# Sums of squares of the head norms in two rounded parts, and gate rows spread by one pass over a high and a low part

## The chip, the cores and the metric

One core of one Trainium2 chip runs the whole program. The metric is the device time of one execution in microseconds (us), as the median of several runs. The engines are TensorE (PE in the profile, its weight loads PEld), VectorE (DVE), ScalarE (ACT), GpSimd (POOL) and SyncE (SP), which here issues nearly all DMAs.

## The reference, cut to what matters

The program is two transformer blocks in a row, on 512 tokens of width 1024. The change touches the places where a vector of one head is divided by its root mean square:

```
def rms_norm(x, g):
    xf = x.astype(jnp.float32)
    y = xf * lax.rsqrt(jnp.mean(xf * xf, axis=-1, keepdims=True) + EPS)
    return (y * g.astype(jnp.float32)).astype(x.dtype)
...
    q = rms_norm(q.reshape(b, nc, CHUNK, N_HEADS, HEAD_DIM), q_norm_g)
    k = rms_norm(k.reshape(b, nc, CHUNK, N_HEADS, HEAD_DIM), k_norm_g)
...
        q_sb = rms_norm_2(to_heads(q_sb, SB_HEADS), g_q_sb[l])
        k_sb = rms_norm_2(to_heads(k_sb, SB_HEADS), g_k_sb[l])
        y_sb = stick_breaking(q_sb, k_sb, to_heads(v_sb, SB_HEADS)).transpose(0, 2, 1, 3)
        y_sb = rms_norm_2(y_sb, g_out_sb[l])
...
        y_ml = rms_norm_2(y_ml.transpose(0, 2, 1, 3), g_out_ml[l]) * jax.nn.sigmoid(o_ml)...
```

The first block has a chunked attention with 16 heads of 64, a gated convolution and a feed-forward part. The second block has two mixers side by side: stick-breaking attention with 8 heads of 64, and an mLSTM with 4 heads of 128, whose weights come from one input gate and one forget gate per head and token. After them comes the PEER layer, which picks 16 of 16384 experts per head and token and is by far the longest part.

## The kernel before, in words

Activations lie with features on partitions and the 512 tokens along the free axis, so one tile is 128 by 512 and holds two heads of 64 or one of 128. Large products (`linear`, `linear2`, `rows_linear`, all through `mm3` at L153 to L155) are made of float32r passes over a rounded high part and a low rest: three matmuls for each product. A float32r operand is made by a cast on ScalarE (`nc.scalar.copy`) and its rest by a subtraction on VectorE or GpSimd (`split` at L180 and L181; `weights` at L142, L144, L148).

The head norms are the exception. `qk_norm` (L494 on) squares a query or key tile on ScalarE (L500, tile `qn_s`) and sums the squares over the 64 rows of each head with one plain float32 matmul against a block matrix of ones (L502, `bone`). `head_norm` (L798 on) does the same for the outputs of the second block's mixers (L803, L805), with `bone` for stick-breaking and a full matrix of ones for the mLSTM. The profile shows each of these float32 matmuls as two PE instructions. The sum lands in the PSUM bank `d`; `rsqrt` (L186 to L200) reads it into `rs_m`, takes Ln and Exp on ScalarE (tile `rs_r`), squares the result (tile `rs_q`) and makes one correction step on VectorE; L504 or L808 then applies it. The tiles `rs_m`, `rs_r`, `rs_q` and `qn_s` have one buffer each in these stages.

There are 32 such sums: four per group in the attention of the first block (4 groups: two query tiles, two key tiles), four per group in stick-breaking (2 groups), four output norms of stick-breaking and four of the mLSTM.

The mLSTM also needs two gate rows per head, spread over all 128 partitions. `gates` makes them for all four heads as tiles of 4 rows (`grow`, `frow`). `products` spreads one row with a float32 matmul against a 0/1 selector of 4 rows (`sel`), at L970 for `grow` and L1012 for `frow`: 8 matmuls in all.

The order of the instructions on each engine is fixed when the program is built: a scheduler of the framework lists them by when it reckons their inputs ready, taking the text's order as priority. On the chip each engine works through its list in that order, and an instruction whose input is late holds up the ones behind it. GpSimd has few jobs in the stages in question: copies of the halves of the q and k tiles (L514), clearing (L605, L922, L984) and the low parts of the mLSTM's q and k (L181).

Of the kernel before, what the change touches and what calls it, by code (L numbers as in the profile page):

```python
# [8 lines left out]
F32 = mybir.dt.float32  # L9
F32R = mybir.dt.float32r  # L10
F16 = mybir.dt.float16
U32 = mybir.dt.uint32
AF = mybir.ActivationFunctionType
# [8 lines left out]
P = 128  # L22
D = 1024
T = 512
# [19 lines left out]
V_QG, V_KG, V_QS, V_KS, V_OSB, V_OML, V_GB = 160, 161, 162, 163, 164, 168, 172  # L44
# [24 lines left out]
class Ker:  # L69
# [12 lines left out]
    def setup(self, es):  # L82
        nc, I = self.nc, self.I
        self.cp = es.enter_context(self.pool("cp"))
        self.raws = None
        self.table, self.table_load, self.table_users = None, None, []
        cst = self.cp.tile([P, 2 * P], F32, name="cst")
        nc.sync.dma_start(cst, I["consts"][:, 0:2 * P])
        vec = self.cp.tile([P, V_W], F32, name="vec")
        nc.sync.dma_start(vec, I["vecs"])  # L90
        self.vec = vec
        self.ident, self.bone = cst[:, 0:P], cst[:, P:2 * P]
        self.ones = self.cp.tile([P, P], F32, name="ones")
        nc.vector.memset(self.ones, 1.0)
        self.mod = self.cp.tile([P, 48], F32, name="mod")

    def act(self, out, x, func, **kw):
# [380 lines left out]
    def gains(self, vcol, mcol):  # L478
# [4 lines left out]
        self.gm = gm  # L483
        return gm

    def qk_in(self, tp, ps, rstd):

        q = tp.tile([P, T], F32, name="qn_n", bufs=2 if rstd is not None else 4)
        if rstd is None:
            self.nc.scalar.copy(q, ps)  # L490
        else:
            self.nc.vector.tensor_mul(q, ps, rstd)
        return q

    def qk_norm(self, tp, pool, q, gcol, tag, twice):


        nc = self.nc
        sq = tp.tile([P, T], F32, name="qn_s", bufs=1)
        nc.scalar.activation(sq, q, AF.Square)  # L500
        pn = self.psum("d" if "d" in self.nbanks else "b")
        nc.tensor.matmul(pn, self.bone, sq, start=True, stop=True)  # L502
        r = self.rsqrt(tp, pn, 1.0 / 64)
        nc.vector.scalar_tensor_tensor(q, q, gcol, r, op0=ALU.mult, op1=ALU.mult)  # L504
        out = []
        for f in range(2):
            own, other = slice(64 * f, 64 * f + 64), slice(64 - 64 * f, 128 - 64 * f)
            a = pool.tile([P, T], F32R, name=f"{tag}a{f}", tag=f"{tag}a{f}")
            nc.scalar.copy(a[own], q[own])
            if twice:  # L510
                b = pool.tile([P, T], F32R, name=f"{tag}b{f}", tag=f"{tag}b{f}")
                nc.vector.tensor_sub(b[own], q[own], a[own].bitcast(F32))
                for t in (a, b):
                    nc.gpsimd.tensor_copy(t[other], t[own])  # L514
                out.append((a, b))
            else:
                nc.vector.tensor_sub(a[other], q[own], a[own].bitcast(F32))
                out.append(a)
        return out
# [137 lines left out]
    def mix(self, es_x):  # L657
        from contextlib import ExitStack
        nc, I = self.nc, self.I
# [7 lines left out]
        tp = self.nq_pool  # L667
# [11 lines left out]
        with ExitStack() as es:  # L679
# [2 lines left out]
            cr = sp.tile([P, 7 * P], F32R, name="cr")  # L682
            self.mlc = sp.tile([P, P], F32, name="mlc")
            nc.sync.dma_start(self.mlc, I["consts"][:, C_MLM:C_MLM + P])
            self.sel = sp.tile([4, 4 * P], F32, name="sel")
            nc.sync.dma_start(self.sel, I["consts"][0:4, C_SEL:C_SEL + 4 * P])
            with self.pool("ci") as tp:
                ci = tp.tile([P, 4 * P], F32, name="ci")
                nc.sync.dma_start(ci, I["consts"][:, C_TRI:C_TRI + 4 * P])
                nc.scalar.copy(cr[:, P:2 * P], ci[:, 0:P])  # L690
                nc.scalar.copy(cr[:, 3 * P:6 * P], ci[:, P:4 * P])
            nc.scalar.copy(cr[:, 0:P], self.ident)
            nc.vector.tensor_scalar_mul(cr[:, 2 * P:3 * P], self.ones, -1.0)
            nc.scalar.copy(cr[:, 6 * P:7 * P], self.ones)
# [63 lines left out]
    def gates(self, sp, hs):  # L758

        nc, I = self.nc, self.I  # L760
        with self.pool("gt") as tp:
            raw = tp.tile([P, KO, P], F32, name="if_w")
            nc.sync.dma_start(raw, I["w_if"])
            hi = tp.tile([P, KO, P], F32R, name="if_h")
            lo = tp.tile([P, KO, P], F32R, name="if_l")
            nc.scalar.copy(hi, raw)
            nc.vector.tensor_sub(lo, raw, hi.bitcast(F32))
            ps = self.linear((hi, lo), 0, hs, tag="b")
            z = tp.tile([P, T], F32, name="if_z")
            nc.scalar.activation(z[:36], ps[:36], AF.Identity, bias=self.v(V_GB)[:36])  # L770
            f = tp.tile([4, T], F32, name="if_f")
            nc.vector.tensor_copy(f, z[32:36])
            e = tp.tile([4, T], F32, name="if_e")
            nc.scalar.activation(e, f, AF.Abs)
            self.act(e, e, AF.Exp, scale=-1.0)
            self.act(e, e, AF.Ln, bias=1.0)
            lf = tp.tile([4, T], F32, name="if_lf")
            nc.vector.scalar_tensor_tensor(lf, f, 0.0, e, op0=ALU.min, op1=ALU.subtract)
            one = tp.tile([4, T], F32, name="if_1")
            nc.vector.memset(one, 1.0)  # L780
            A = tp.tile([4, T], F32, name="if_A")
            nc.vector.tensor_tensor_scan(A, one, lf, 0.0, op0=ALU.mult, op1=ALU.add)
            b = tp.tile([4, T], F32, name="if_b")
            nc.vector.tensor_sub(b, z[0:4], A)
            grow = sp.tile([4, T], F32, name="grow")
            nc.vector.tensor_tensor_scan(grow, one, b, 0.0, op0=ALU.mult, op1=ALU.max)
            frow = sp.tile([4, T], F32, name="frow")
            nc.vector.tensor_add(frow, A, grow)
            self.act(frow, frow, AF.Exp, scale=-1.0)
            nc.vector.tensor_scalar_min(frow, frow, 1e18)  # L790
            pb = self.psum("b")
            for s in range(4):
                nc.tensor.transpose(pb[:, 4 * s:4 * s + 4], b[:, s * P:(s + 1) * P], self.ident[:4, :4])
            bt = sp.tile([P, 16], F32, name="bt")
            nc.vector.tensor_copy(bt, pb[:, :16])
        return bt, grow, frow

    def head_norm(self, tp, mp, y, ones, gcol, scale, eps=None, extra=None):  # L798


        nc = self.nc
        sq = tp.tile([P, T], F32, name="qn_s", bufs=1)
        nc.scalar.activation(sq, y, AF.Square)  # L803
        pn = self.psum("d")
        nc.tensor.matmul(pn, ones, sq, start=True, stop=True)  # L805
        r = self.rsqrt(tp, pn, scale, eps=eps)
        t = tp.tile([P, T], F32, name="hn_t", bufs=1)
        nc.vector.scalar_tensor_tensor(t, y, gcol, r, op0=ALU.mult, op1=ALU.mult)  # L808
# [4 lines left out]
    def stick_breaking(self, mp, hs, pq, pk):  # L813
        nc, I = self.nc, self.I
        widths = [512, 384, 256, 256]
        out = []
        with self.pool("sb") as tp, self.pool("sbq", bufs=2) as qp, self.pool("sbv", bufs=4) as vp:
# [53 lines left out]
            def head(g, j, f, qk, vs):  # L871
# [9 lines left out]
                    ys[g, j] = tp.tile([P, T], F32, name="sb_y", bufs=1)  # L881
                self.weigh_values(ys[g, j], f, self.psum("d"), vs, 2 * j + f, ws, widths)
                if f:
                    out.append(self.head_norm(tp, mp, ys[g, j], self.bone, self.v(V_OSB + 2 * g + j), 1.0 / 64))
                yield

            old = None
# [59 lines left out]
    def mlstm(self, mp, tp, qp, vp, ml, bt, grow, frow):  # L947
# [69 lines left out]
        def norm(h, pn, den):  # L1017
# [5 lines left out]
            self.act(l, l, AF.Ln, bias=1.0)  # L1023
            nc.vector.scalar_tensor_tensor(o, o, 0.0, l, op0=ALU.min, op1=ALU.subtract)
            self.act(o, o, AF.Exp)
            return self.head_norm(tp, mp, pn, self.ones, self.v(V_OML + h), 1.0 / P, den, o)

        for h in range(4):
            yield [norm(h, *products(h))]
# [498 lines left out]
```

## Time and profile before

| | |
|---|---|
| median of 3 runs | 2579.02 us (2578.01 to 2582.98) |
| profiled execution: its own time | 2575.19 us |
| profiled execution: span | 2573.4 us |
| mean granted TensorE clock | 0.992 |
| PE busy | 2489.6 us (97%) |
| DVE busy | 1898.0 us (74%) |
| ACT busy | 1100.5 us (43%) |
| POOL busy | 617.4 us (24%) |

The span runs from the first to the last instruction; the time of the profiled execution is 1.8 us longer. The attention of the first block lies at about 190 to 505 us, the second block's mixers at about 950 to 1290 us, and the PEER layer from there to the end. Matmuls are pipelined: an entry's duration holds the way through the array, so what one matmul costs PE is read from the distance between starts.

### The profile page before, as it was taken

How to read it: one execution, taken by the hardware profiler on the slowest of the kernel's cores; microseconds unless marked ns; L12 is line 12 of the kernel's file. 1: busy time of each engine (PE TensorE's matmuls, PEld its weight loads, DVE VectorE, ACT ScalarE, POOL GpSimd, SP SyncE). 2: the span in 40 equal slices, each digit the busy share in tenths (PEclk: the TensorE clock that was granted, in tenths of full speed). 3: DMA queues.
4: the chain of work that ended last, by engine and by line, in shares of the span. 5: the costliest groups of instructions: out<-in, count | busy, mean ns of one | idle time of the engine just before them, and what ended most of it. 6: DMA issues, size and time to landing. Idle time of an engine off the chain costs nothing.

```text
span 2573.4 us, 33226 instructions
## 1 busy us (share of the span) xinstructions
PE 2489.6 (97%) x12637; PEld 2118.3 (82%) x12637; DVE 1898.0 (74%) x3238; ACT 1100.5 (43%) x1479; POOL 617.4 (24%) x510
## 2 busy tenths in 40 slices
PE   8999999999999999999999979989999999999999
PEld 6887877877888878777788967868889999999998
DVE  5558777745555567887789989847767777888887
ACT  4226555633222247657643248733333333333332
POOL 0001110111001101101054420001135555555552
PEclk9999999999999999999999989989999999999999
DMA  5352222444444331134333357689879999999995
GB/s 194 128 203 95 101 86 99 170 150 142 161 164 147 131 119 67 58 105 142 131 121 109 119 183 275 266 274 348 298 262 328 326 332 328 328 333 331 331 332 192
DMA packets 172313, 515.04 MB, mean 200 GB/s; under 512 B 13396, under 2 KB 78308, under 8 KB 146296
## 3 DMA queue, kind: packets, MB, share of 16 engines
q1 hardware_dynamic: 133960, 376.52, 41.7%
q0 software_dynamic: 37040, 135.35, 14.6%
q8 instruction: 99, 1.62, 0.2%
q10 hardware_dynamic: 1152, 1.05, 0.1%
q14 instruction: 62, 0.51, 0.1%
HBM read 461.47 MB, written 51.38 MB: 199 GB/s over the span
## 4 chain that ended last, share of the span: by engine, by line
PE 76%; DVE 14%; ACT 5%; issue 2%; DMA 2%; POOL 1%; SPq 0%; DVEq 0%; ACTq 0%; POOLq 0%
PE pa L155 12%; PE pa L153 11%; PE pa L154 11%; PE pp L1417 7%; PE pp L1416 7%; PE pp L1420 7%; PE pu L153 4%; PE pu L155 4%; PE pu L154 4%; ACT whi L142 1%; DVE wlo L144 1%; DVE tk_rest L1187 1%; PE pb L588 1%; PE pc L608 1%; DMA mg_a<-g_dram 1%
## 5 line engine op out<-in xcount | busy, mean ns | idle before, releaser
L142 ACT CAST whi<-wraw 128x2048 fp32r<-128x2048 f32 x229 | 437.7, 1911 | 573.0 <-PE pa L154 295.7
L144 DVE TENSOR_TENSOR wlo<-wraw,whi 128x2048 fp32r<-128x2048 f32 x210 | 492.8, 2346 | 139.0 <-ACT whi L142 134.3
L155 PE MATMUL pa<-hh,wlo 128*128 128x512 f32 (+1 forms) x1360 | 521.8, 385 | 19.8 <-POOL wlo L148 17.2
L153 PE MATMUL pa<-hh,whi 128*128 128x512 f32 (+1 forms) x1360 | 526.4, 387 | 14.9 <-ACT hh L228 10.8
L154 PE MATMUL pa<-lh,whi 128*128 128x512 f32 (+1 forms) x1360 | 523.1, 385 | 0.0
L155 PEld LDWEIGHTS pa<-hh,wlo 128*128 128x128 f32 x1360 | 257.7, 190 | 65.0 <-POOL wlo L148 18.9
L153 PEld LDWEIGHTS pa<-hh,whi 128*128 128x128 f32 x1360 | 258.0, 190 | 61.9 <-ACT hh L228 11.3
L1416 PE MATMUL pp<-whi,hew 128*128 128x512 f32 x768 | 300.1, 392 | 6.4 <-ACT hew L1383 6.4
L1417 PE MATMUL pp<-wlo,hew 128*128 128x512 f32 x768 | 300.6, 392 | 1.6 <-DVE wlo L144 1.6
L1145 POOL DMA_INDIRECT r_row<-in_u_rows,r_at x128 | 186.0, 1453 | 479.5 <-DVE r_w L1166 447.3
L154 PEld LDWEIGHTS pa<-lh,whi 128*128 128x128 f32 x1360 | 258.0, 190 | 44.2 <-issue 6.5
L1420 PE MATMUL pp<-whi,lew 128*128 128x512 f32 x768 | 237.6, 391 | 0.0
L1145 POOL DMA_INDIRECT r_row<-in_expert_v,r_at x128 | 194.9, 1522 | 177.1 <-DVE r_big L1174 139.5
L153 PE MATMUL pu<-hh,whi 128*128 128x384 f32 x640 | 217.0, 339 | 0.0
L155 PE MATMUL pu<-hh,wlo 128*128 128x384 f32 x640 | 216.7, 339 | 0.0
L154 PE MATMUL pu<-lh,whi 128*128 128x384 f32 x640 | 216.3, 338 | 0.0
L1416 PEld LDWEIGHTS pp<-whi,hew 128*128 128x128 f32 x768 | 144.6, 188 | 35.7 <-ACT hew L1383 6.6
L1417 PEld LDWEIGHTS pp<-wlo,hew 128*128 128x128 f32 x768 | 144.4, 188 | 30.4 <-DVE wlo L144 2.5
L1420 PEld LDWEIGHTS pp<-whi,lew 128*128 128x128 f32 x768 | 144.5, 188 | 30.4
L1174 DVE SCALAR_TENSOR_TENSOR r_big<-r_row,r_w,r_big 128x1024 f32<-128x1024 f32 x127 | 162.9, 1283 | 3.0
L1383 ACT CAST hew<-ex_w 128x384 fp32r<-128x384 f32 x128 | 65.6, 513 | 228.3 <-DVE ex_w L1379 151.3
L1166 DVE CUSTOM_DVE_ANT_0 r_row<-r_row,r_big 128x1024 f32<-128x1024 f32 x128 | 151.4, 1220 | 0.0
(436 smaller groups left out, 4552.5 us busy)
## 6 DMA issues: line engine op xcount, KB each, us to landing
wraw<-in_expert_u SPq DMA_DIRECT2D x64, 1024.0 KB, 7.2
wraw<-in_expert_v SPq DMA_DIRECT2D x64, 1024.0 KB, 7.6
wraw<-in_w_in SPq DMA_DIRECT2D x37, 1024.0 KB, 4.8
ada_w<-in_w_ada SPq DMA_DIRECT2D x24, 1024.0 KB, 4.8
gate_dram<-oh_s SPq DMA_DIRECT2D x12, 2048.0 KB, 6.9
ex_g<-gate_dram SPq DMA_DIRECT2D x31, 768.0 KB, 9.9
wraw<-in_w_up SPq DMA_DIRECT2D x16, 1024.0 KB, 5.9
wraw<-in_w_down SPq DMA_DIRECT2D x16, 1024.0 KB, 4.8
```

The costliest lines, as they stand in the source:

```text
L142: nc.scalar.copy(hi, raw)
L144: nc.vector.tensor_sub(lo, raw, hi.bitcast(F32))
L153: mm(out, wh, xh, start=start, stop=False)
L154: mm(out, wh, xl, start=False, stop=False)
L155: return mm(out, wl, xh, start=False, stop=stop)
L1145: self.nc.gpsimd.indirect_dma_start(t, None, src, at)
L1166: later(nc.vector.tensor_tensor_reduce(row, row, h, 1.0, 0.0, op0=ALU.mult, op1=ALU.add, accum_out=w[:, k:k + 1]))
L1174: later(nc.vector.scalar_tensor_tensor(acc, row, w[:, k:k + 1], acc, op0=ALU.mult, op1=ALU.add))
L1383: nc.scalar.copy(hi, w)
L1416: mm(sums[b][half], hi, v[0][:, c, hc], start=n == 0, stop=False)
L1417: mm(sums[b][half], hi, v[1][:, c, hc], start=False, stop=False)
L1420: mm(sums[b][half], lo, v[0][:, c, hc], start=False, stop=n == P - 1)
```

## The change

Every sum of squares goes through a new method `sum_squares`: the squares (`qn_s`) are cast to float32r on ScalarE (`hi`), GpSimd subtracts to get the rest (`lo`), and two float32r matmuls add both parts in the bank. `hi` and `lo` take the buffers of `rs_m` and `rs_q`, which `rsqrt` uses afterwards. The matrices of ones are float32r copies (`boner`, new, made at the start; `onesr`, which was there). The two gate rows become tiles of 36 rows: the rounded rows on partitions 0 to 3, the rest on 32 to 35, zeros elsewhere, and the selector has ones at both places, so that one float32r matmul spreads a row.

```
@@ setup
+        self.boner = self.cp.tile([P, P], F32R, name="boner")
+        nc.scalar.copy(self.boner, self.bone)
...
+    def sum_squares(self, tp, q, ones, tag):
+        nc = self.nc
+        sq = tp.tile([P, T], F32, name="qn_s", bufs=1)
+        hi = tp.tile([P, T], F32R, name="qn_h", tag="rs_m")
+        nc.scalar.activation(sq, q, AF.Square)
+        nc.scalar.copy(hi, sq)
+        lo = tp.tile([P, T], F32R, name="qn_l", tag="rs_q")
+        nc.gpsimd.tensor_sub(lo, sq, hi.bitcast(F32))
+        pn = self.psum(tag)
+        nc.tensor.matmul(pn, ones, hi, start=True, stop=False)
+        nc.tensor.matmul(pn, ones, lo, start=False, stop=True)
+        return pn
@@ qk_norm
-        sq = tp.tile([P, T], F32, name="qn_s", bufs=1)
-        nc.scalar.activation(sq, q, AF.Square)
-        pn = self.psum("d" if "d" in self.nbanks else "b")
-        nc.tensor.matmul(pn, self.bone, sq, start=True, stop=True)
+        pn = self.sum_squares(tp, q, self.boner, "d" if "d" in self.nbanks else "b")
@@ mix
-            self.sel = sp.tile([4, 4 * P], F32, name="sel")
-            nc.sync.dma_start(self.sel, I["consts"][0:4, C_SEL:C_SEL + 4 * P])
+            self.sel = sp.tile([36, 4 * P], F32R, name="sel")
...
+                cs = tp.tile([36, 4 * P], F32, name="cs")
+                nc.vector.memset(cs, 0.0)
+                for p in (0, 32):
+                    nc.sync.dma_start(cs[p:p + 4], I["consts"][0:4, C_SEL:C_SEL + 4 * P])
+                nc.scalar.copy(self.sel, cs)
@@ gates
-            grow = sp.tile([4, T], F32, name="grow")
+            grow = tp.tile([4, T], F32, name="if_g")
...
-            frow = sp.tile([4, T], F32, name="frow")
+            frow = tp.tile([4, T], F32, name="if_r")
...
-        return bt, grow, frow
+            out = []
+            for n, x in (("g", grow), ("f", frow)):
+                both = sp.tile([36, T], F32R, name=f"{n}row")
+                nc.gpsimd.memset(both.bitcast(F32), 0.0)
+                nc.scalar.copy(both[0:4], x)
+                nc.vector.tensor_sub(both[32:36], x, both[0:4].bitcast(F32))
+                out.append(both)
+        return bt, *out
@@ head_norm
-        sq = tp.tile([P, T], F32, name="qn_s", bufs=1)
-        nc.scalar.activation(sq, y, AF.Square)
-        pn = self.psum("d")
-        nc.tensor.matmul(pn, ones, sq, start=True, stop=True)
+        pn = self.sum_squares(tp, y, ones, "d")
```

The callers of `head_norm` pass `boner` and `onesr` in place of `bone` and `ones`.

## Rows read from the trace of the kernel before

**Rows 1.** Busy time of each engine by stretch: attention, norms, stick-breaking, mLSTM.
```profile
core 0: us, PE busy (x) PEld busy (x) DVE busy (x) ACT busy (x) POOL busy (x), PEclk, DMA share, GB/s
190.00:505.00 315.00, 309.38 (x1633) 252.05 (x1632) 245.49 (x534) 180.66 (x353) 33.35 (x62) 1.00 0.31 107
950.00:1000.00 50.00, 49.94 (x268) 40.55 (x267) 36.08 (x50) 28.41 (x46) 7.27 (x10) 1.00 0.25 86
1000.00:1140.00 140.00, 129.41 (x676) 107.40 (x676) 124.44 (x210) 101.11 (x175) 9.37 (x13) 0.98 0.16 55
1140.00:1290.00 150.00, 142.58 (x692) 111.06 (x691) 112.32 (x166) 92.90 (x164) 12.60 (x14) 1.00 0.42 142
```

**Rows 2.** Tile qn_s: counts, duration ns min/median/max, first and last start.
```profile
L502 PE MATMUL pd<-qn_s,cst x48: 590/592/697, 196.8 to 1072.9; 128*128 128x512 f32 x48
...
L805 PE MATMUL pd<-qn_s,cst x8: 590/592/697, 1035.5 to 1134.4; 128*128 128x512 f32 x8
...
L805 PE MATMUL pd<-qn_s,ones x8: 590/592/594, 1193.5 to 1244.0; 128*128 128x512 f32 x8
```

**Rows 3.** Tile sel, in the same columns.
```profile
L970 PE MATMUL pg<-grow,sel x8: 587/640/692, 1170.0 to 1226.6; 4*128 4x512 f32 x8
```

**Rows 4.** Timeline of PE around one sum of the attention: start, duration, instruction.
```profile
363.29 0.39 PE L153 MATMUL pa<-hh,whi 128*128 128x512 f32 x1
363.54 1.13 PE L502 MATMUL pd<-qn_s,cst 128*128 128x512 f32 x2
364.10 0.80 PE L154 MATMUL pa<-lh,whi 128*128 128x512 f32 x1
364.74 0.39 PE L155 MATMUL pa<-hh,wlo 128*128 128x512 f32 x1
364.96 0.39 PE L153 MATMUL pa<-hh,whi 128*128 128x512 f32 x1
```

**Rows 5.** Timeline of PE around one sum of stick-breaking.
```profile
993.27 0.40 PE L153 MATMUL pa<-hh,whi 128*128 128x512 f32 x1
...
994.59 0.39 PE L155 MATMUL pa<-hh,wlo 128*128 128x512 f32 x1
```

**Rows 6.** Timeline of PE around one spread gate row.
```profile
1191.22 0.28 PE L155 MATMUL pa<-whi,lh 128*128 128x256 f32 x1
1191.43 1.12 PE L1012 MATMUL pd<-frow,sel 4*128 4x512 f32 x2
...
1192.70 0.28 PE L154 MATMUL pa<-wlo,hh 128*128 128x256 f32 x1
```

**Rows 7.** Groups by shape on POOL and ACT: busy, mean ns, idle before.
```profile
L181 POOL TENSOR_TENSOR lk<-ml_a,hk 128x512 fp32r<-128x512 f32 x4 | 6.1, 1514 | 22.0 <-ACT hk L180 21.8
L181 POOL TENSOR_TENSOR lq<-ml_a,hq 128x512 fp32r<-128x512 f32 x4 | 5.7, 1425 | 33.1 <-ACT hq L180 33.1
...
L180 ACT CAST hmx<-hn_t 128x512 fp32r<-128x512 f32 x8 | 5.0, 619 | 9.9 <-DVE hn_t L808 5.2 <-DVE hn_t L810 4.8
```

**Rows 8.** Waits of PE, 190 to 510 us: total, times, longest.
```profile
PE pd L502 <- ACT qn_s L500: 1.7, 5, 0.8
```

**Rows 9.** Waits of PE, 1140 to 1290 us.
```profile
PE ps L155 <- POOL lk L181: 0.7, 1, 0.7
PE ps L153 <- ACT hk L180: 0.6, 1, 0.6
```

**Rows 10.** Timelines of DVE and POOL beside each other near 997 us.
```profile
997.86 0.98 DVE L200 SCALAR_TENSOR_TENSOR rs_q<-rs_q,rs_r 128x512 f32<-128x512 f32 x1
...
1002.81 0.69 DVE L197 SCALAR_TENSOR_TENSOR rs_q<-rs_m,rs_q 128x512 f32<-128x512 f32 x1
...
997.34 1.97 POOL L514 CAST qb<-qb 64x512 fp32r<-64x512 f32 x2
```

**Rows 11.** Timeline of DVE: the norms of the first group of the attention.
```profile
211.93 0.68 DVE L189 TENSOR_SCALAR rs_m<-pd 128x512 f32<-128x512 f32 x1
212.53 0.74 DVE L504 SCALAR_TENSOR_TENSOR qn_n<-qn_n,gq,rs_q 128x512 f32<-128x512 f32 x1
...
219.99 0.74 DVE L504 SCALAR_TENSOR_TENSOR qn_n<-qn_n,vec,rs_q 128x512 f32<-128x512 f32 x1
```

**Rows 12.** Timelines of POOL and PE at the group's first scores.
```profile
223.21 1.63 POOL L514 CAST kb<-kb 64x512 fp32r<-64x512 f32 x2
...
227.65 0.28 PE L588 MATMUL pb<-ka,qa 128*128 128x256 f32 x1
```

More of the change, by code (lines that the diff above doesn't have):

```diff
@@ L883, in head @@
                 if f:
-                    out.append(self.head_norm(tp, mp, ys[g, j], self.bone, self.v(V_OSB + 2 * g + j), 1.0 / 64))
+                    out.append(self.head_norm(tp, mp, ys[g, j], self.boner, self.v(V_OSB + 2 * g + j), 1.0 / 64))
                 yield
@@ L1025, in norm @@
             self.act(o, o, AF.Exp)
-            return self.head_norm(tp, mp, pn, self.ones, self.v(V_OML + h), 1.0 / P, den, o)
+            return self.head_norm(tp, mp, pn, self.onesr, self.v(V_OML + h), 1.0 / P, den, o)
         for h in range(4):
```

## The prediction

> **What bounds the kernel now.** I read the busy times first, then the same by stretch, then the two tiles the change is about, then PE's timeline around single instructions, and last the waits. The reader should see in the stretches that PE is what every touched stage is full of: 309.4 of 315 us in the attention, 49.9 of 50 while the first norms of stick-breaking run, 142.6 of 150 in the mLSTM [rows 1]. Only the stretch from 1000 to 1140 is different: PE is busy for 129.4 of 140 us and DVE for 124.4, so there PE waits some 10.6 us for chains that run over DVE and ACT. After 1290 us nothing is changed; what comes before shifts it as a whole, so that a microsecond won or lost before 1290 counts in full.
>
> **What PE is spared.** There are 48 + 8 + 8 PE instructions for the sums [rows 2], two for each, so 32 sums; and 8 for one kind of gate row [rows 3], two for each of four heads, the other kind being the same again: 8 rows. The price of a float32 sum is read from starts. In the attention a float32r pass goes out every 0.22 to 0.23 us (364.74 to 364.96). From the pass ahead of the sum to the second pass behind it there are 1.45 us (363.29 to 364.74) [rows 4]; less two ordinary passes (0.46) the sum costs 0.99 us, its slow successor of 0.80 us included. In stick-breaking the same distance is 1.32 us [rows 5], so 0.86. The new form costs two passes, 0.46 us. Sixteen sums lie in the attention and sixteen in the second block: 16 x (0.99 - 0.46) + 16 x (0.86 - 0.46) = 8.5 + 6.4 = 14.9 us.
>
> A gate row takes 1.48 us from the short pass ahead (1191.22) to the second behind [rows 6]; less two short passes of half the columns (0.11 each, half of 0.23) that is 1.26. The new row is one pass, 0.23 us, but over 36 of 128 rows. The old one costs 0.27 to 0.40 more than a sum over all rows, so something may hang on the narrow shape and stay: 0.23 to 0.63. I take 0.5, since the new shape is nearly as narrow: 8 x 0.76 = 6.1 us (bounds 5.0 and 8.2). Together 21.0 us of PE work go away.
>
> **What is added.** Each sum gets a cast of 128x512 on ACT, 0.62 us, and a subtraction of 128x512 on POOL, 1.43 to 1.51 us by the low parts of the mLSTM's q and k [rows 7]. ACT's 32 x 0.62 = 20 us are spread over stages where it is busy for 57 to 72% [rows 1], and POOL's 32 x 1.47 = 47 us over stages where it has 7 to 15%. Their throughput is free; were ACT's cover gone, all 20 us would count. What is not free is the order. A sum's result used to be there 1.13 us after its square was [rows 4]; now it takes 0.62 + 1.47 and a last pass of 0.39, so 2.5 us, 1.35 us later.
>
> *Waits of PE for the new links.* PE now waits at the place of `hi` for ACT and at the place of `lo` for POOL. Queued behind are `linear`'s passes, which need nothing of it; they are the cover if the scheduler puts the passes late enough. No row shows this sum in two parts. Below, it costs nothing; above, if PE stood for both links, 2.1 us, 67 us in all. The nearest rows are the mLSTM's q and k: the same cast, the same subtraction on POOL, and PE passes that need them. There PE waited 0.7 us for POOL once and 0.6 for ACT once, in 8 such pairs [rows 9], 0.16 us for each. The square itself, in the attention, cost PE 1.7 us in 16 sums [rows 8], 0.11 each. I take 0.16: 32 x 0.16 = 5.1 us.
>
> *DVE beside POOL.* While POOL copies 64x512 (997.34 to 999.31), DVE's step at 997.86 takes 0.98 us; the same shape alone takes 0.69 [rows 10]: 0.29 longer. A subtraction of 1.47 us can lie beside two such steps, so up to 0.6 us of DVE. In the attention DVE has 70 us to spare [rows 1] and this hides. Between 1000 and 1140 it doesn't: four q and k norms and four output norms lie there, 8 x 0.6 = 4.6 us above, nothing below if they fall beside steps that don't suffer. I take the middle, 2.3 us.
>
> The page SBUF — State Buffer of the Trainium skill (section "Who interferes with whom") speaks against the change more strongly: DVE and GpSimd share a port pair as an exclusive lock, an instruction with two SBUF inputs on DVE contends with GpSimd's reads, and whoever is first blocks the other for a whole instruction. The trace shows 0.29 us where a whole copy would be about 1 us [rows 10], so it bears out the contention, not the full lock. By the rule the eight subtractions would hold DVE 8 x 1.47 = 11.8 us; by the row, 2.3 to 4.6.
>
> *The small edits.* `boner` is one ACT cast at the start, when ACT waits for the first inputs; `sel` gets one DMA more on SP, a memset and a cast, in a stretch where PE has its list full (49.9 of 50). The gate rows add one ACT cast and one DVE subtraction each ahead of the first spread, with some 0.62 + 0.69 us once by [rows 7, 10]; behind it are the mLSTM's first weights. Between 1140 and 1290 PE idles 7.4 us as it is, so between 0 and 1.3 us; I take 0. The POOL memsets come early.
>
> **Sum.** 21.0 - 5.1 - 2.3 = 13.6 us off the profiled 2575.19 us: 2561.6 us. The median of the runs lies 3.8 us above the profiled time, so I forecast 2579.0 - 13.6 = 2565.4 us, about 0.5% faster.
>
> **The rivals.** *All of it arrives.* If PE's list has room for every new link and DVE doesn't suffer, 21 us stay: 2558 us. For it speaks that PE is over 98% busy in the attention; against it, that between 1000 and 1140 a shorter PE has nothing to do with the spare time.
>
> *The norms queue up behind each other.* `hi` and `lo` sit in the one buffer of `rs_m` and of `rs_q`, and `rs_q` is free only when the norm ahead has been applied. Before, the first key's sum was read at 211.93, ahead of the end of the norm before it (212.53 + 0.74 = 213.27) [rows 11]. Now its low part can't be written before that norm is applied, which itself is 1.35 us later: 214.6, and with the subtraction and the pass the reading starts near 216.5, 4.6 us later. The rest of that norm took until 219.99, 8 us for some 4 us of steps, so up to 4 us may be caught up. The first scores start 2.8 us after the last copy they need (223.21 + 1.63 = 224.84 to 227.65) [rows 12]. If nothing is caught up, 1.8 us are lost in each of six groups, 11 us: 2565.4 + 11 = 2576 us, no change. Against it: V's products and gate products are there for PE to fill with, which is why I leave it out of the sum.
>
> *The full lock.* By the whole-instruction block the eight subtractions of the stretch 1000 to 1140 would cost 11.8 us of DVE, not 2.3: 2575 us, no change. This is the mechanism of the cited section; the rows speak for a fifth to two fifths of it.
>
> *Slower.* PE stands at `lo`. PE's list is written by the scheduler's reckoning; if that takes POOL for faster than it is, `lo` is listed too early and all passes behind it stand. The attention's four groups are in the same order, so one bad place comes four times. From 21.0 / 32 = 0.66 us per sum on, the change loses. With 1.0 us, less than the subtraction alone, PE stands for 32 us: 2579 + 32 - 21 = 2590 us. PE's wait of 0.8 us for a square [rows 8] shows that single waits of this size occur; that it was one in sixteen, and 0.16 us per pair with POOL [rows 9], speaks against it.
>
> **Chances.** The forecast 0.50 (2561 to 2573), all of it 0.15, the queue of norms 0.13, the full lock 0.07, slower 0.15. What a measurement here can tell from no change is about 0.2%, 5 us: below 2574 is faster, above 2584 slower. The two cases in the middle straddle that edge: I give 0.07 of their 0.20 to faster and 0.13 to no change. So faster 0.72, same 0.13, slower 0.15. The range reaches from a little under the full gain to what no change with a little stall gives, 2555 to 2581, and leaves out the slower case and a bit at either end.
>
> **What would show it.** In the changed kernel PE's starts around a high or low pass should lie 0.23 us apart with no slow successor. The attention should shrink by 5 to 8 us and the rest up to 1290 us by 6 to 12. The waits of PE should name POOL's subtraction (`qn_l`) with some 0.1 to 0.2 us per sum: over 0.66 us means the slower case. DVE's idle time for `rs_m` should grow by over 1 us per norm without PE's growing. DVE steps beside a subtraction should take near 1.0 us, not 2. I am wrong above all if the order on PE, which is made anew, puts `lo` in front of work that was ready, or if the first scores of each group come 2 us later against V's last product.

## The result

The changed kernel takes 2600.68 us (median of 4 runs, 2599.02 to 2605.92) against 2579.2 us before (4 runs): a ratio of 1.0084, 95% interval 1.0066 to 1.0102. It is 0.84% slower. I had forecast 2565.4 us, a range of 2555 to 2581 and slower at 0.15; the time lies outside the range and on the other side. The profiled execution has a span of 2599.3 us and a mean clock of 0.985, so 25.9 us and 0.007 away from before. Behind the mixers hardly anything moved: from the PEER layer's first pass to the end it is 1296.8 us before and 1297.8 in the changed kernel.

First the busy times by stretch, the same stretches as in [rows 1], and behind them three stretches of 2 us that come up again below:

```profile
core 0: us, PE busy (x) PEld busy (x) DVE busy (x) ACT busy (x) POOL busy (x), PEclk, DMA share, GB/s
190.00:505.00 315.00, 300.40 (x1589) 247.51 (x1589) 244.61 (x527) 187.17 (x364) 56.10 (x78) 0.99 0.28 95
950.00:1000.00 50.00, 49.26 (x269) 40.56 (x267) 34.85 (x46) 30.32 (x47) 6.77 (x9) 1.00 0.27 94
1000.00:1140.00 140.00, 128.39 (x641) 106.33 (x640) 117.33 (x187) 98.66 (x170) 22.02 (x25) 0.94 0.15 53
1140.00:1290.00 150.00, 131.81 (x649) 105.41 (x649) 111.05 (x170) 93.55 (x171) 21.42 (x20) 0.95 0.34 116
...
284.00:286.00 2.00, 0.53 (x2) 0.48 (x3) 1.94 (x3) 0.00 (x0) 1.42 (x1) 1.00 0.43 74
286.00:288.00 2.00, 2.00 (x7) 1.58 (x6) 1.28 (x2) 0.65 (x2) 0.00 (x0) 0.66 0.90 373
288.00:290.00 2.00, 2.00 (x6) 1.52 (x5) 0.69 (x1) 0.63 (x2) 0.00 (x0) 0.50 0.19 78
```

PE, which was full in the attention (309.4 of 315 us busy), now idles there for 14.6 us, and between 1140 and 1290 us for 18.2 of 150. POOL has the new subtractions: 56.1 us in the attention where it had 33.4 [rows 1]. VectorE is busy there for 244.6 us against 245.5, so GpSimd's new work doesn't show as a loss of VectorE's there. And the granted clock is lower from 1000 us on, 0.94 and 0.95 against 0.98 and 1.00. Who PE waits for is in its waits (three stretches: 186 to 520, 1000 to 1145, 1140 to 1310; total us, times, longest):

```profile
PE pd L499 <- POOL qn_l L496: 11.4, 13, 1.9
...
PE pd L499 <- POOL qn_l L496: 6.6, 8, 2.2
PE pd L555 <- DVE sb_wh L884: 2.9, 1, 2.9
...
PE pd L555 <- DVE sb_wh L884: 3.7, 1, 3.7
PE pg L991 <- DVE grow L818: 2.9, 1, 2.9
...
PE pd L499 <- POOL qn_l L496: 1.0, 3, 0.5
```

L499 is the pass over `lo` (tile `qn_l`), L496 GpSimd's subtraction. In [rows 8, 9] no wait for a sum was of this size. The wait for `sb_wh`, a part of stick-breaking's weights, isn't new; before it was, from 1000 to 1145:

```profile
PE pd L542 <- DVE sb_wh L863: 5.8, 2, 3.4
```

The same from the side of the tile, for the whole span of the changed kernel:

```profile
L496 POOL TENSOR_TENSOR qn_l<-qn_s,qn_h x32: 1273/1288/2854, 196.3 to 1274.1; 128x512 fp32r<-128x512 f32 x32
...
its engine sat idle before it (us, times) until:
  ACT qn_h L494: 225.5, 18
  DVE qn_n L517: 62.9, 10
...
  DVE ml_u L517: 15.8, 2
...
who waited for it (us, times):
  PEld pd L499: 27.6, 25
  DVE rs_m L191: 25.9, 10
  PE pd L499: 18.6, 23
  ACT qn_s L493: 6.1, 7
```

PE stood 18.6 us for `lo`, in 23 of 32 sums. Twelve of the 32 subtractions (10 + 2) could start only when the norm ahead had been applied (L517), because `lo` takes the one buffer of `rs_q`. The subtraction alone takes 1.28 us; its longest is 2.85. One sum of the attention, and from 1083.81 on one norm of the second block, in order of time, other rows between them left out:

```profile
281.91 0.62 ACT L494 CAST qn_h<-qn_s 128x512 fp32r<-128x512 f32 x1
282.01 2.28 DVE L146 TENSOR_TENSOR wlo<-wraw,whi 128x2048 fp32r<-128x2048 f32 x1
282.58 0.50 PE L498 MATMUL pd<-qn_h,boner 128*128 128x512 f32 x1
282.61 2.81 POOL L496 TENSOR_TENSOR qn_l<-qn_s,qn_h 128x512 fp32r<-128x512 f32 x1 [6.50 <-ACT qn_h L494]
282.92 0.39 PE L156 MATMUL pa<-lh,whi 128*128 128x512 f32 x1
283.15 0.40 PE L157 MATMUL pa<-hh,wlo 128*128 128x512 f32 x1
285.47 0.50 PE L499 MATMUL pd<-qn_l,boner 128*128 128x512 f32 x1 [1.93 <-POOL qn_l L496]
...
286.81 0.63 PE L156 MATMUL pa<-lh,whi 128*128 128x512 f32 x1
287.24 0.63 PE L157 MATMUL pa<-hh,wlo 128*128 128x512 f32 x1
...
1083.81 0.74 DVE L517 SCALAR_TENSOR_TENSOR qn_n<-qn_n,gqs,rs_q 128x512 f32<-128x512 f32 x1
1084.72 1.29 POOL L496 TENSOR_TENSOR qn_l<-qn_s,qn_h 128x512 fp32r<-128x512 f32 x1 [0.61 <-DVE qn_n L517]
1086.04 0.63 ACT L493 ACTIVATE qn_s<-qn_n 128x512 f32<-128x512 f32 x1 [0.20 <-POOL qn_l L496]
1086.06 0.49 PE L499 MATMUL pd<-qn_l,boner 128*128 128x512 f32 x1 [0.49 <-POOL qn_l L496]
1092.93 0.68 DVE L199 SCALAR_TENSOR_TENSOR rs_q<-rs_m,rs_q 128x512 f32<-128x512 f32 x1
1093.64 0.62 ACT L494 CAST qn_h<-qn_s 128x512 fp32r<-128x512 f32 x1 [1.43 <-DVE rs_q L199]
```

In the first part PE has `lo` two ordinary passes behind `hi`, 0.46 us of work, while the subtraction takes 2.81 us because VectorE's big subtraction (L146, two inputs from SBUF) began 0.6 us ahead of it; PE stands 1.93 us with ready passes behind. In the next two stretches the granted clock is 0.66 and 0.50, and the passes go out 0.43 us apart and not 0.23. Three of the attention's four groups have this same collision, with 1.92 us of standing each: 5.8 of the 11.4 us. In the second part the chain of a norm runs through its own buffers: the application frees `rs_q` for `lo`, the subtraction frees `qn_s` for the next square, and the cast into `rs_m` waits for L199 of the norm ahead.

A table of stages helps with the experiments. Its borders are starts in the timelines: the attention runs from the first scaled query to the first output pass over its result, "to the mixers" from there to the first matmul of the second block's input norm, "mixers" from there to PEER's first pass. Idle and clock are PE's after 190 us, summed over stretches of 2 us up to 1320: the time it was not busy, and one minus the granted clock, times the length.

| kernel | span | attention | to mixers | mixers | idle | clock |
|---|---|---|---|---|---|---|
| before | 2573.4 | 301.4 | 449.0 | 330.8 | 29.0 | 3.4 |
| changed | 2599.3 | 311.3 | 448.6 | 347.5 | 50.8 | 18.7 |

So the attention lost 9.9 us and the mixers 16.7, where I had forecast 5 to 8 and 6 to 12 as gains.

### The profile page after: what moved, and what is told of

Its sections match the earlier page's. It is cut to its first block, busy times and chain, and to the rows that moved or that the text cites. A ratio compares the mean times of both kernels' runs of the same rounds, so it can differ in the third digit from the quotient of the medians.

```text
span 2599.3 us, 33266 instructions
## 1 busy us (share of the span) xinstructions
PE 2493.8 (96%) x12629; PEld 2129.3 (82%) x12629; DVE 1911.2 (74%) x3241; ACT 1125.5 (43%) x1515; POOL 664.8 (26%) x544
## 4 chain that ended last, share of the span: by engine, by line
PE 74%; DVE 14%; ACT 5%; POOL 2%; issue 2%; DMA 2%; SPq 0%; DVEq 0%; POOLq 0%; ACTq 0%
PE pa L155 12%; PE pa L157 12%; PE pa L156 11%; PE pp L1438 7%; PE pp L1441 7%; PE pp L1437 7%; PE pu L155 4%; PE pu L157 4%; PE pu L156 4%; ACT whi L144 1%; POOL qn_l L496 1%; DVE wlo L146 1%; DVE tk_rest L1208 1%; DMA mg_a<-g_dram 1%; ACT oh_s L1345 1%
## 5 line engine op out<-in xcount | busy, mean ns | idle before, releaser
L146 DVE TENSOR_TENSOR wlo<-wraw,whi 128x2048 fp32r<-128x2048 f32 x210 | 492.7, 2346 | 134.1 <-ACT whi L144 129.6
## 6 DMA issues: line engine op xcount, KB each, us to landing
ex_g<-gate_dram SPq DMA_DIRECT2D x31, 768.0 KB, 11.4
```

## The experiments

Three theories stood at the beginning, the first two being rivals of the prediction. **A:** PE stands at `lo`, which its list puts too close behind `hi`, because GpSimd is later than the list reckons. **B:** the norms queue up in the single buffers of `rs_m`, `rs_q` and `qn_s`. **C:** GpSimd's reads slow VectorE. C has little for it in the busy times above. Later a fourth came up: PE's spared time is worth nothing where PE doesn't set the end.

**The low part by VectorE.** A subtraction there takes 0.69 us and not 1.28 to 2.85.

```
-        nc.gpsimd.tensor_sub(lo, sq, hi.bitcast(F32))
+        nc.vector.tensor_sub(lo, sq, hi.bitcast(F32))
```

> The changed kernel with the subtraction for the low part on VectorE in place of GpSimd; all else as it is. Theory A (PE stands at the low pass, because it is listed some two passes, 0.5 us, behind the high pass while GpSimd needs 1.3 to 2.8 us): PE's waits for the low part fall from about 20 us to under 5, the granted clock stays up, and the time comes below that of the kernel before, 2565 to 2575 us. Theory B (the norms queue up behind the one buffer that the low part shares): the buffers are the same, so the time stays near 2595 us or above. Theory C (GpSimd's reads slow VectorE): without GpSimd the time falls as in A.

Measured: 2603.28 us, ratio 1.0087 (1.0064 to 1.011); attention 300.2, to mixers 457.2, mixers 352.3. PE's waits of the attention (186 to 520), then 1000 to 1145:

```profile
PE pa L155 <- DVE qn_n L508: 4.3, 4, 1.1
...
PE pd L498 <- ACT qn_h L494: 0.8, 1, 0.8
...
PE pd L499 <- DVE qn_l L496: 1.7, 3, 1.2
```

No wait for `lo` is left in the attention, and its 11 us are back: there the loss is PE's stand at GpSimd's `lo`, as A says. The run takes away GpSimd's usual lateness and its collisions with VectorE together and doesn't tell the two apart; the trace does, by the 5.8 of 11.4 us above. The total is no better than the change's, against A's 2565 to 2575 us. VectorE pays with its own order: PE now waits four times, 4.3 us, for the scaled input of a norm (L508). The mixers are slower still than in the change (352.3 against 347.5), with hardly a wait for `lo`: there A is not the cause. The new 8 us between the two come further down.

**Only the gate rows.** All 32 sums are float32 again (the lines of before in `qk_norm` and `head_norm`, with `bone` and `ones`); the gate rows and `sel` stay as changed.

```
-        pn = self.sum_squares(tp, y, ones, "d")
+        sq = tp.tile([P, T], F32, name="qn_s", bufs=1)
+        nc.scalar.activation(sq, y, AF.Square)
+        pn = self.psum("d")
+        nc.tensor.matmul(pn, ones, sq, start=True, stop=True)
```

> The kernel before with the gate rows' part of the change alone; the sums of squares are float32 matmuls as before. All theories put the loss in the sums, so this part alone should give 0 to 6 us: 2573 to 2580 us. If the wait of 2.9 us for the first spread row, which the changed kernel shows, belongs to this part, it gives back half of the gain: about 2577 us. Over 2590 us would mean that the gate rows are the cause.

Measured: 2579.18 us, ratio 0.9995 (0.9982 to 1.0007). The gate rows neither win nor lose. From one (1191.22) to the next pass (1191.65) there are 0.43 us; measured as the prediction measured the old row, from the pass ahead (1217.98) to the second behind (1219.07) less two ordinary passes (0.46), a new row costs 0.63 us. That is the dear end of the range where I took 0.5, and PE is spared 8 x 0.63 = 5.0 us. This doesn't come out at the end: from 1140 to 1290 the granted clock is 0.98 in this kernel against 1.00 before, some 3 us.

**The low part made but not added.**

```
-        nc.tensor.matmul(pn, ones, hi, start=True, stop=False)
-        nc.tensor.matmul(pn, ones, lo, start=False, stop=True)
+        nc.tensor.matmul(pn, ones, hi, start=True, stop=True)
```

> The changed kernel without the matmul over the low part; GpSimd still makes the low part, but nobody reads it (the sums leave out the rest of the rounded squares). Theory A: PE has nothing to stand at, so the time falls below that of the kernel before by the PE work spared, some 20 to 28 us: 2550 to 2562 us. Theory B: the low part still has its turn in the shared buffer, but nothing waits for it on PE; the queue of norms stays in part: 2580 us or more. Theory C (GpSimd beside VectorE costs the time): GpSimd's work is all there, so the time stays near 2590 us or above.

Measured: 2594.68 us, ratio 1.0051 (1.0037 to 1.0066); attention 305.4, mixers 342.1. PE's waits from 186 to 520 show that the stand has moved one link ahead, to ScalarE's cast:

```profile
PE pd L498 <- ACT qn_h L494: 10.4, 13, 1.2
```

A's 2550 to 2562 us is missed by far, and the time alone would allow B and C. But the stand shows that it isn't GpSimd alone: in the order of this kernel, PE's list puts the last pass of a sum too early for whatever comes last ahead of it.

**`lo` in a buffer of its own** (that of `gz` in the attention, of `hn_t` in the mixers).

```
-        lo = tp.tile([P, T], F32R, name="qn_l", tag="rs_q")
+        own = dict(tag="gz", bufs=2) if "c" in self.nbanks else dict(tag="hn_t", bufs=1)
+        lo = tp.tile([P, T], F32R, name="qn_l", **own)
```

> The changed kernel with the low part in a buffer that lies idle at that time (that of the gate products in the attention, that of the output norms in the second block), no longer in the one of the correction step. The low pass is then listed 2 or 3 passes behind the high one nearly everywhere. Theory A: PE stands there for all 32 sums, some 0.8 us or more for each, so PE's waits for the low part rise to 25 us or more and the time stays at 2598 to 2610 us. Theory B: the queue of norms is gone and the time falls to 2590 us or below.

Measured: 2611.02 us, ratio 1.0115 (1.0093 to 1.0137); attention 314.7, mixers 348.6. B's 2590 us or below is missed. PE's waits for `lo` come to 19.9 us in the whole span, near the change's 18.6 and under A's 25. The attention isn't helped by taking `lo` out of `rs_q`, which speaks against B there. The mixers aren't helped either, but here `hi` still sat in `rs_m`, and in the mixers `lo` shared a buffer with the output norms.

**Both parts of the q and k sums in pairs of idle buffers**, once with GpSimd, once with VectorE. The function takes the two names and the number of buffers, and q and k pass them on:

```
+        where = ("at_e3", "gz") if "c" in self.nbanks else ("sb_w", "sb_l")
-        pn = self.sum_squares(tp, q, self.boner, "d" if "d" in self.nbanks else "b")
+        pn = self.sum_squares(tp, q, self.boner, "d" if "d" in self.nbanks else "b", where, 2)
```

> The changed kernel with both parts of the 24 q and k sums in pairs of buffers that lie idle at that time (those of the last exponentials and of the gate products in the attention, of the weights and logarithms in stick-breaking), so that nothing of a sum shares a buffer with the correction step. Theory B, in the form that the second block's four norms take 50 us from the first query's square to the last one applied, where it was 33, because high part, low part and square each wait for the norm ahead: the norms overlap again, those 17 us shrink to under 6, and the time falls by 8 to 15 us to 2585 to 2593 us. Theory A alone (PE stands at the low pass, listed too early): the low pass is listed 2 to 4 passes behind the high one, PE stands for each, and the time stays at 2598 to 2612 us.

> As the run with both parts moved, and the low part made by VectorE. If A and B together are the cause, both are taken away here: PE's waits for the low part under 5 us, the second block's four norms in under 38 us, and a time below that of the kernel before, 2565 to 2576 us. If VectorE, which is full in stick-breaking, now sets the pace, 2580 to 2590 us. Over 2595 us both theories are wrong or something else is in the way.

Measured: GpSimd 2604.51 us, ratio 1.0089 (1.0073 to 1.0106); attention 316.3, mixers 339.8. VectorE 2598.8 us, 1.0077 (1.006 to 1.0093); attention 300.6, to mixers 458.0, mixers 330.8. The last of the second block's q and k norms was applied 161.5 us after the mixers' start in the changed kernel, at 142.9 and 145.6 us here, 139.9 before: the queue is gone with its buffers, and the mixers get 8 us back with GpSimd and, set beside the run with VectorE and single buffers, 21.5 with VectorE (352.3 to 330.8). So B holds in the second block, though neither total falls as far as expected. In the attention PE still stands at GpSimd's `lo` (first line, 186 to 520, of the kernel with GpSimd):

```profile
PE pd L499 <- POOL qn_l L496: 12.6, 13, 1.9
```

The kernel with VectorE has neither of the losses, and yet is at 1.0077. Of the 20.8 us by which its span is longer than before, 9.0 are between the two (458.0 against 449.0), in the merge behind the attention, and 12.7 lie behind the mixers: from PEER's first pass to the end it takes 1309.5 us against 1296.8. PE's waits from 488 to 620, and the longest behind the mixers, there first of this kernel, then of the kernel before:

```profile
PE pa L155 <- ACT hm L384: 4.6, 1, 4.6
...
PE pa L157 <- POOL wlo L150: 22.3, 5, 9.4
...
PE pa L155 <- POOL wlo L148: 17.2, 3, 9.5
```

The merge's last high part starts at 550.59 us, 545.48 before, PE waits 4.6 us for it (0.7 before), and the clock costs 4.9 us there (0 before). Behind the mixers PE waits 5.1 us longer for the low parts of weights that GpSimd makes (`wlo`). None of the change's code runs in these two stages; their order on the engines is made anew with every edit. Why it comes out worse here I didn't settle. It also shows what a new order alone can do to a stage.

**Which sums lose.** One kernel has the 24 sums of q and k in float32 again, so that only the eight output norms and the gate rows are new; one has the second block's eight q and k sums in float32 again.

```
-        pn = self.sum_squares(tp, q, self.boner, "d" if "d" in self.nbanks else "b")
+        sq = tp.tile([P, T], F32, name="qn_s", bufs=1)
+        nc.scalar.activation(sq, q, AF.Square)
+        pn = self.psum("d" if "d" in self.nbanks else "b")
+        nc.tensor.matmul(pn, self.bone, sq, start=True, stop=True)
```

> The changed kernel with the 24 q and k sums back to one float32 matmul; the 8 sums of the output norms and the gate rows stay changed. Theories A and B both put the loss in the q and k sums (A also a little in the output norms): 2572 to 2582 us. Over 2588 us would mean that the output norms carry it.

> The changed kernel with the 8 q and k sums of the second block back to one float32 matmul; the 16 of the attention, the output norms and the gate rows stay changed. The attention's 10 us stay. Theory B for the second block: its 16 to 17 us go, 2584 to 2590 us. If the second block's loss were spread over the output norms and gate rows: 2592 to 2600 us.

Measured: output norms alone 2586.4 us, ratio 1.0031 (1.0021 to 1.0042), mixers 340.2. Without the second block's q and k 2594.61 us, ratio 1.0058 (1.0042 to 1.0075), attention 311.0, mixers 338.4. Both came out worse than the theories had it, and the second is in the range that I had given for a loss spread over the output norms and gate rows. So eight output norms alone lose some 8 us of the mixers (331.9 with the gate rows alone), the second block's q and k another 9 (347.5 - 338.4), the attention's 16 sums 10.

**PE's work without the links.** The square is rounded by the activation itself, so that cast, subtraction and buffers fall away; in one kernel it is passed twice, PE's work of the change, in the other once. Both leave out the low part of the squares, and with two passes the sums come out doubled.

```
-        sq = tp.tile([P, T], F32, name="qn_s", bufs=1)
-        hi = tp.tile([P, T], F32R, name="qn_h", tag="rs_m")
+        sq = tp.tile([P, T], F32R, name="qn_s", bufs=1)
         nc.scalar.activation(sq, q, AF.Square)
-        nc.scalar.copy(hi, sq)
-        lo = tp.tile([P, T], F32R, name="qn_l", tag="rs_q")
-        nc.gpsimd.tensor_sub(lo, sq, hi.bitcast(F32))
         pn = self.psum(tag)
-        nc.tensor.matmul(pn, ones, hi, start=True, stop=False)
-        nc.tensor.matmul(pn, ones, lo, start=False, stop=True)
+        nc.tensor.matmul(pn, ones, sq, start=True, stop=False)
+        nc.tensor.matmul(pn, ones, sq, start=False, stop=True)
```

> As the run with one pass, but the same rounded square is passed twice: PE's work is that of the change exactly, and the cast and the subtraction are gone (the sums come out doubled; the low part is left out). Against the change this takes away the new links and nothing else. If the prediction's term for PE is right and only the links cost, 14.9 us come off: about 2564 us. With the smaller saving that the starts in the changed kernel show (0.25 to 0.5 us for each sum) 8 to 16 us: 2563 to 2571. If PE's spared time is worth nothing by itself, 2574 to 2584, and the links of the change cost the 21 us between that and 2600.

> Every sum takes its square rounded straight by the activation (128x512 written as float32r) and one pass over it: no cast, no subtraction, no low part, no second pass, and no new buffers. What is left out is the low part of the squares; the gate rows are spread as in the change. So PE is spared more than by the change, and nothing is added ahead of it. If the spared passes are worth their time by starts, 0.99 - 0.23 = 0.76 us in the attention and 0.86 - 0.23 = 0.63 in the second block, 16 of each give 22 us: about 2557 us, and the change's loss comes from its links alone. If the ends of the touched stretches are set by chains over ACT and DVE whatever PE is spared, the time stays within 5 us of 2579.

Measured, beside 2581.3 us of before on the same chip: two passes 2577.96 us, ratio 0.9989 (0.998 to 0.9997); one pass 2567.04 us, ratio 0.9951 (0.9938 to 0.9964). This is the run that decides most. With PE's work of the change and no links, 3 us are won of the 21 that I had put down for PE; that is the case in which PE's spared time is worth nothing by itself (2574 to 2584 us). One pass gives 14 us, between the two cases that I had named (2557, or within 5 us of 2579). Where they went, in the table's terms:

| kernel | span | attention | to mixers | mixers | idle | clock |
|---|---|---|---|---|---|---|
| two passes | 2572.9 | 294.6 | 451.5 | 335.7 | 36.7 | 10.2 |
| one pass | 2562.1 | 292.5 | 451.4 | 325.8 | 32.7 | 10.2 |

With two passes the attention got 6.8 us shorter, the stretch to the mixers 2.5 and the mixers 4.9 longer. (With the links and VectorE the attention had 300.2, so 5.6 of the 6.8 are lost to the links even then.) The stretch 1000 to 1140 of the kernel with two passes, to be set beside its row in [rows 1]:

```profile
1000.00:1140.00 140.00, 125.76 (x657) 105.75 (x655) 125.58 (x214) 99.86 (x173) 10.49 (x15) 0.95 0.15 51
```

PE is busy for 3.6 us less in it, VectorE for 1.1 more, and the clock is 0.95 where it was 0.98. From before to two passes the span fell by 0.5 us, while idle time and clock loss grew by 7.7 and 6.8: some 15 us of PE work went away, and as much came in as standing and slow clock. From two passes to the change it rises by 26.4 us (22.7 by the medians), with 14.1 more of idle and 8.5 more of clock; this is what the cast, the subtraction and their buffers cost, with the new order that comes with them.

**Output norms with the low part by VectorE.** The kernel with the output norms alone, with this line:

```
-        nc.gpsimd.tensor_sub(lo, sq, hi.bitcast(F32))
+        nc.vector.tensor_sub(lo, sq, hi.bitcast(F32))
```

> The 24 sums of q and k are one float32 product as before; the eight output norms and the gate rows have the new form, with the low part made by VectorE in place of GpSimd. With GpSimd this was 2586.4 us. If GpSimd's lateness (1.3 to 2.85 us for a subtraction that PE's list places right behind) is what these eight lose, most of the 7 us goes: 2578 to 2582. If it is the longer chain itself, in a stretch that has no cover, it stays at 2584 to 2588.

Measured: 2580.51 us, ratio 1.0004 (0.9995 to 1.0013), mixers 334.2. With GpSimd gone the eight output norms lose hardly anything (1.0031 to 1.0004). The longest waits of PE from 1000 to 1310, first of the kernel with GpSimd:

```profile
PE pd L499 <- POOL qn_l L496: 4.2, 4, 2.0
PE pd L558 <- DVE sb_wh L887: 4.0, 2, 3.7
PE pd L498 <- ACT qn_h L494: 3.6, 1, 3.6
```

and of that with VectorE, where neither `lo` nor `hi` is among them:

```profile
PE pd L558 <- DVE sb_wh L887: 6.7, 2, 3.4
PE ps L155 <- ACT hk L182: 3.2, 1, 3.2
```

**Only the second block's q and k**, in pairs of buffers of their own, low part by GpSimd; all else but the gate rows in float32.

```
+        if "c" in self.nbanks:
...
+        else:
+            pn = self.sum_squares(tp, q, self.boner, "d" if "d" in self.nbanks else "b", ("sb_w", "sb_l"), 2)
```

> Only the eight q and k sums of the second block and the gate rows have the new form, with both parts in pairs of buffers of their own and the low part by GpSimd; attention and output norms are as before. If the queue in the buffers was all that these eight lost, then they are now free of it and bring 8 x 0.25 to 0.5 us: 2575 to 2577 us. If PE stands at the low part here too, as in the attention, 0.6 us for each: 2584 us. If neither shows, 2579.

Measured: 2578.9 us, ratio 0.9994 (0.9985 to 1.0003), mixers 332.0. Free of the queue these eight sums lose nothing, and they win nothing either, though by starts PE is spared some 8 x 0.4 us.

## Why the prediction was wrong

Forecast were 13.6 us of gain, measured are 21.5 of loss. Some 18 us of the difference are spared PE time that didn't arrive (3.3 of 21.0, by the two passes without links), some 15 are the links, 22.7 us by the medians where the sum had 5.1 + 2.3. The sum had no term at all for the clock, whose loss up to 1320 us grew from 3.4 to 18.7 us.

*PE is spared 21 us.* By starts this was near. Counted over the sums with full passes on either side, the distance that I read as 0.99 in the attention has a median of 0.995 before and 0.605 with two passes (12 sums each); in the second block 0.89 (8) and 0.475 (10). A mean of 1.18 against 0.75 in the attention gives 16 x 0.43 = 6.9 us, and its stage fell by 6.8. The gate rows' share was 5.0 us, not 6.1. The step that failed is that the second block's 6.4 us and the gate rows' 6.1 were put into the sum at full value. From 1000 to 1140 VectorE had been at 124.4 of 140 us and PE idle for 10.6 [rows 1]; I used that against the rival in which all arrives, and left the 12.5 us in the sum all the same. The two passes without links, the gate rows alone and the second block's q and k alone each show that nothing of them comes out at the end. For the mLSTM, where PE was busy for 142.6 of 150 us [rows 1], VectorE's share isn't the reason, and it stays open. Nor is the value nothing in every order: with one pass the mixers take 325.8 us, 5.0 less than before.

*PE waits 5.1 us for the links.* It was 18.6 us at `lo`, 0.58 per sum and not 0.16. The row that I took the price from [rows 9] had the same subtraction, but in another place of the list. In the attention PE stands in 13 of 16 sums, and the last three groups repeat nearly the same stands, much as the slower rival said. Taking `lo` from GpSimd ended it there (attention 311.3 to 300.2) and with the output norms (1.0031 to 1.0004).

*The slower rival, PE stands at `lo`*, is what happened in the attention and at the output norms, but its edge was wrong: 0.66 us per sum, since it set the stand against 21 us of gain. With 3 us of gain it is 3 / 32, some 0.1 us. And the stand brings more than itself: between the two passes and the change, clock loss adds 8.5 us to 14.1 of idle.

*The norms queue up.* I placed this in six groups, four of them in the attention, and gave it 11 us. In the attention it cost nothing that shows: with VectorE and the single buffers it takes 300.2 us, with VectorE and pairs of buffers 300.6. It came in the second block, some 8 us, through `rs_m` and `qn_s` as well as `rs_q`, and pairs of buffers ended it.

*DVE beside POOL, 2.3 us, and the full lock.* The contention is there, but it is GpSimd that pays, and PE behind it. Seven of the 32 subtractions took over 1.3 us (2.81 three times, 2.85, 2.39, 1.66, 1.47), and each of the seven began while a VectorE operation with two inputs from SBUF was running, with 0.34 to 1.73 us of it left: each lasted this rest and 1.12 to 1.16 us more. Eight others began while VectorE ran an operation with an input in PSUM (`vv<-pa`, `sb_l<-pb`, `x<-pa`, `ml_d<-pd`) and took 1.27 to 1.30 us. In the sum shown above VectorE's ran from 282.01 to 284.29 and GpSimd's from 282.61 to 285.42. By the Trainium skill's page SBUF — State Buffer (section "Who interferes with whom") whichever comes first blocks the other for a whole instruction. This trace agrees here. PE's stands behind four of them make 8.0 of the 18.6 us at `lo`; by an estimate from the rows, 1.8 would be left of these had the four lasted 1.28 us. VectorE was caught too, in this pair:

```profile
1234.09 2.39 POOL L496 TENSOR_TENSOR qn_l<-qn_s,qn_h 128x512 fp32r<-128x512 f32 x1 [3.84 <-ACT qn_h L494]
1235.25 1.78 DVE L183 TENSOR_TENSOR lmx<-hn_t,hmx 128x512 fp32r<-128x512 f32 x1
```

VectorE's subtraction of 128x512, behind GpSimd's, took 1.78 us, where I had expected near 1.0 and not 2; alone it takes 0.68. So the rival of the full lock, at 0.07, had the mechanism, with the price on the other engine. The copy in [rows 10], by which I took a fifth to two fifths of it, was misread. The row merges two copies; the first alone reads

```profile
997.34 0.95 POOL L514 CAST qb<-qb 64x512 fp32r<-64x512 f32 x1
```

It ended at 998.29, 0.43 us after VectorE's step at 997.86 had begun. Only so much of it was left to block the step, which took 0.29 us longer: that is no sign against the lock.

*The small edits at nothing.* PE stood 2.9 us once for the first gate row (`grow`) in the change, where I took 0 of 0 to 1.3. Alone with float32 sums the gate rows cost nothing at the end.

The 26 us of the span (21.5 by the medians) thus come from three places: 10 in the attention (PE at `lo`, and the clock), 8 to 9 in the second block's q and k (the queue), 8 in the output norms (PE at `lo` and `hi`, and the clock), with the spared PE time unseen in the last two. Three things stay open: why the merge loses 8 to 9 us with the low part on VectorE, why the PEER layer loses 12.7 in one of these kernels, and why one pass less shortens the mixers by 9.9 us where PE's work falls by 16 x 0.23 = 3.7. The engines' order is made anew for each kernel, and I have no run that holds it fixed. So a new order by itself remains a rival wherever two kernels differ by a few us; the stands at `lo` and the queue are seen in the traces themselves.

## What to carry to other kernels

Put a spared microsecond of an engine into the sum only for a stage whose end that engine sets; where another is as busy and the engine already waits, price it at nothing until a run without the new links shows otherwise. A split into high and low parts puts two links on other engines ahead of a product, here a cast on ScalarE and a subtraction on GpSimd, and the list that the scheduler makes can place the second pass too early: count the place of each new pass against the slowest duration of its maker, not the usual one. Of all versions only the two without links have an interval that lies below the kernel before. One pass over squares that the activation rounds itself gives 0.9951, and it gives up the low part of the squares; two passes give 0.9989.

## What was not expected of the hardware

A stand of PE can be paid again in its clock, but isn't each time. After the 1.93 us at 283.5 to 285.5 the granted clock was 0.66 and 0.50 over the next two stretches of 2 us, at passes without a gap, which costs 0.68 + 1.00 = 1.7 us more. The second of the attention's three equal stands, up to 365.09, is followed by 0.78, 0.50 and 0.87 from 364 on, again 1.7 us. After the third, 1.92 us up to 445.24, nothing falls:

```profile
446.00:448.00 2.00, 2.00 (x10) 1.64 (x9) 1.21 (x3) 0.89 (x2) 0.00 (x0) 1.00 1.01 426
```

Likewise a stand of 2.9 us for `hh`, near 590 us, is followed by a fall in the kernel with two passes and by none in the kernel before or in the change. Up to 1320 us the kernel before lost 3.4 us to the clock, the change 18.7.
